# A hybrid attention block on one core: one gating weight's cast placed behind the cast of the keys' second slice

## The chip, the core and the metric

The kernel runs on one core of a Trainium2 chip. The core has five engines that run their own instruction streams: PE (TensorE, matrix products), DVE (VectorE), ACT (ScalarE), POOL (GpSimd) and SP (SyncE, which here only issues transfers). They wait for each other through semaphores, and each works through its own instructions strictly in the order in which they were built. The metric is the device time of one execution in microseconds (us); lower is better. A program was profiled once per version, and the profile is a record of one execution.

## The reference, cut to what matters

The layer projects 512 positions and 16 leading "meta" positions (528 in all) with one large weight `w_in`, runs two causal attention branches with 16 heads each beside each other, gates both and merges them.

```
u = rmsnorm(h)
proj = u @ w_in          # cq, ckv, k_pe, z_mla, fq, fk, fv, f_logit, z_fox, gate_a, gate_b
o_mla = attention(q_m, k_m, v_mla)                 # latent branch
y_mla = (o_mla * silu(z_mla)) @ w_br_mla
cum   = cumsum(log_sigmoid(f_logit + b))
o_fox = attention(fq, fk, fv, cum)                 # forgetting branch
y_fox = (o_fox * silu(z_fox)) @ w_br_fox
h = h + rmsnorm((sig(gate_a)*y_mla + sig(gate_b)*y_fox) @ w_out)
```

## The kernel before, in words

**Two-part products.** Every matrix product is done in three passes, since each fp32 operand is held as a rounded part (`h`) and a remainder (`l`): high by high, high by low, low by high. A weight slab of 128 x 1024 is loaded into `wraw`, ACT rounds it into `wh` (line 127, in `wsplit`), and POOL subtracts to get `wl` (line 102). The pools of `wraw`, `wh` and `wl` hold three slabs each, so a new load starts only when an older slab's `wl` is done, and a new cast only when PE has used an older `wh` for the last time. The same split is made of activations: ACT rounds (line 239, in `hl_done`) and DVE subtracts (line 102).

**Stages.** Heads are taken in pairs. There are 16 attention stages: for each pair `pr` from 0 to 7 first the forgetting branch (`br` = 1), then the latent branch (`br` = 0). PE is filled in all of them: while DVE and ACT work on the softmax of a stage, PE computes the projections that the next stages need (the list `fill`). A stage consists of `s0` (scores of the query blocks 0, 1, 2), the attention-times-values product `ov` of the stage before (`late`), `s1` (scores of block 3), and then the steps of `fill` with the softmax parts `n0` and `n1` among them. For a forgetting stage the list is: one transposing transfer of the values, eight steps of its own gate `z_unit(1, pr)`, two of the latent queries `mq`, four of the latent gate `z_unit(0, pr)`, and so on; the twelfth step, `fill[11]`, is the first one of the latent gate, and it is this step that calls for the cast of the latent gate's weight. For a latent stage the list ends with the second slice of the next forgetting stage's keys `fk` (columns 272 to 527), right before that stage's `s0`.

**Order.** PE runs in the order written in the program. For ACT, DVE and POOL a scheduler at build time sets the order from priorities, and may pull an instruction far ahead of the place where it is written. `tc.issue_after(x)` tells the scheduler that an instruction must stand behind `x` on its engine; the list `behind` holds such an `x` for the casts in `wsplit`, and `halved[key, i]` remembers the cast of slice `i` of a stage's queries or keys. Transfers are all issued by SP, one after the other: weight loads, the transposing transfers of the softmax numerators (`pt<-pn`, eight in each stage) and of the values (`vp<-vh`), and small loads.

In the scores of `s0`, block 0 reads keys 0 to 143 (matmuls of 144 columns), block 1 keys 0 to 271, block 2 keys 0 to 399. So the first two need the first slice of the keys alone, and the third, with 400 columns, is the first reader of the second slice: its rounded part from ACT, and for the last two of its six key matmuls the remainder from DVE. DVE reads the finished scores out of PSUM (line 755), ACT takes exponentials (line 763), ACT and DVE scale and split them (lines 790, 791).

Of the kernel before, what the change touches and what calls it, by code (L numbers as in the profile page):

```python
# [54 lines left out]
def block_kernel(ctx: ExitStack, tc: tile.TileContext, x, meta_tokens, pre_norm_g, w_in, fox_forget_b,  # L55
# [29 lines left out]
    behind, through, first_t, exps, halved = [], [], [], [], {}  # L85
# [126 lines left out]
    def run(steps):  # L212
        for _, fn in steps:
            fn()
# [309 lines left out]
    def gate_unit():  # L524

        i, br = gates.pop(0)

        def done(_, ps):
            ths[i, br] = thp.tile([128, S], F32, tag="th", name=f"th{i}{br}")
            nc.scalar.activation(ths[i, br], ps, AF.Tanh, scale=0.5)  # L530
        return unit(f"pg{i}{br}", win_w((O_GA, O_GB)[br], i), u_act, KD, REAL, done)


    with ExitStack() as att:
# [289 lines left out]
        def feed(br, pr):  # L824

            q = (q_mla, q_fox)[br](pr)
            k = (k_mla, k_fox)[br](pr)
            v, vts[br, pr] = v_unit(br, pr)
            return q, k, v
# [13 lines left out]
        for si, (br, pr) in enumerate(stages):  # L843
            last = si + 1 == len(stages)
            if not last:
                q, k, v = feed(*stages[si + 1])
            if br == 1:

                za, zb = z_unit(1, pr), z_unit(0, pr)
                fill = (vts[br, pr] if pr else begun) + za + q + zb[:4] + k + zb[4:6] + v + zb[6:]  # L850
            elif not last:

                fill = vts[br, pr] + q + k[:KD] + v + k[KD:]
            else:
                g = gate_unit()
                fill = vts[br, pr] + g + gate_unit() + gate_unit()
# [9 lines left out]
        for si, (br, pr) in enumerate(stages):  # L866
            s0, s1, n0, n1, va = attention(br, pr)

            for fn in [s0] + late + [s1]:
                fn()  # L870

            fill = fills[si]
            if si == 0:

                run(fill[:5])
                run(vts[1, 0] + pe_rest)
                n0()
                n1()
                first_t.extend(through)
                run(fill[5:])  # L880
            else:
                run(fill[:1])
                if si == 1:

                    written[0] = True
                    for x in range(2):
                        store0(x, 2, 8)
                    written[0] = False
                run(fill[1:5])
                if si == 1:  # L890

                    behind[:] = exps[:1]
                if si == 2:
                    behind.clear()
                n0()
                run(fill[5:12])
                n1()
                if 6 <= si < 8:

                    written[0] = True  # L900
                    rest1(si - 6)
                    written[0] = False
                run(fill[12:])
            written[0] = False
            if si == 1:

                behind[:] = [halved[("k", 1, 1), 0]]
            late = [va]
# [146 lines left out]
```

## Time and profile before

| what | value |
|---|---|
| median of 3 runs | 625.7 us (625.54 to 627.62) |
| span of the profiled execution, first to last instruction | 622.1 us |
| PE busy | 599.9 us, 96% of the span |
| ACT busy | 330.8 us, 53% |
| DVE busy | 315.4 us, 51% |
| POOL busy | 265.5 us, 43% |
| attention stages | about 67 us to 421 us of the span |

The profile page gives a span for the profiled execution and no other time of its own; the median of the runs is 3.6 us above that span, which holds what lies ahead of the first and behind the last instruction of the program. A timeline row of the profile reads: start in us from the span's start, duration, engine, line, operation, output tile <- input tiles with shapes, count, and in brackets the time for which the engine sat idle just before it and what ended that wait. A row of the chain of waits reads: start, duration, what the time belongs to.

### The profile page before, as it was taken

To read this page: it belongs to the slowest core of one execution; us is meant where nothing else is said; L and a number is where in the kernel's file an instruction comes from. 1 tells how busy PE (TensorE), PEld (TensorE's weight loads), DVE (VectorE), ACT (ScalarE), POOL (GpSimd) and SP (SyncE) were. 2 spreads that over 40 slices of the span, in tenths; PEclk is the share of its full clock that TensorE was granted. 3 is DMA by queue.
4 is the path that set the end of the run, shared out by engine and by line. 5 is a ranking of instruction groups with operands and counts; after the bars stand their busy time and mean duration, and the time that the engine had idled before them with its cause. 6 is when DMAs were issued, how large, how long until landed. Compare 5 with 4: busy or idle time off the path is not lost.

```text
span 622.1 us, 11008 instructions
## 1 busy us (share of the span) xinstructions
PE 599.9 (96%) x3811; PEld 507.3 (82%) x3811; DVE 315.4 (51%) x922; ACT 330.8 (53%) x757; POOL 265.5 (43%) x270
## 2 busy tenths in 40 slices
PE   5997999799999999999999999999999999999996
PEld 5886789689889789888888898887888888888885
DVE  3848647555765764674675657627321122024034
ACT  7755745655764864774676657656322222232321
POOL 4307535352346543344443523542744444444610
PEclk9999999899999999999999999999999999999999
DMA  9422589969798787878579697871433332333602
GB/s 289 99 76 53 120 178 142 242 141 190 145 186 161 149 208 154 172 167 204 140 161 174 145 169 159 187 168 40 136 102 101 102 93 79 100 103 115 257 34 102
DMA packets 223512, 89.31 MB, mean 144 GB/s; under 512 B 141708, under 2 KB 216852, under 8 KB 223456
## 3 DMA queue, kind: packets, MB, share of 16 engines
q1 hardware_dynamic: 223456, 88.61, 61.9%
q8 instruction: 30, 0.49, 0.3%
q14 instruction: 26, 0.21, 0.1%
HBM read 54.43 MB, written 4.00 MB: 94 GB/s over the span
## 4 chain that ended last, share of the span: by engine, by line
PE 86%; DVE 5%; ACT 4%; issue 2%; DMA 1%; SPq 0%; POOL 0%; DVEq 0%; ACTq 0%
PE z L96 14%; PE pg L96 14%; PE py L96 14%; PE v L96 9%; PE fq L96 7%; PE po L96 7%; PE fk L96 7%; PE st L96 5%; PE ov L96 3%; PE psm L96 3%; DVE sf L755 2%; PE mq L96 2%; ACT wh L127 2%; PE mk L96 1%; DVE vh L690 1%
## 5 line engine op out<-in xcount | busy, mean ns | idle before, releaser
L102 POOL TENSOR_TENSOR wl<-wraw,wh 128x1024 fp32r<-128x1024 f32 (+1 forms) x90 | 207.3, 2308 | 221.0 <-ACT wh L127 219.2
L127 ACT CAST wh<-wraw 128x1024 fp32r<-128x1024 f32 (+1 forms) x90 | 89.9, 1003 | 172.3 <-issue 47.7
L763 ACT ACTIVATE sf<-sf,nb 128x144 f32<-128x144 f32 (+3 forms) x128 | 72.0, 564 | 15.8 <-DVE nb L755 15.8
L791 DVE SCALAR_TENSOR_TENSOR pn<-sf,ri,pn 128x128 f16<-128x128 f32 (+3 forms) x128 | 68.8, 576 | 13.1 <-ACT pn L790 12.2
L790 ACT ACTIVATE pn<-sf,ri 128x128 f16<-128x128 f32 (+3 forms) x128 | 61.5, 551 | 19.9 <-ACT sf L763 17.9
L938 DVE SCALAR_TENSOR_TENSOR tb<-th,py 128x512 f32<-128x512 f32 x16 | 11.0, 687 | 101.9 <-PE py L96 101.9
L96 PE MATMUL st<-hlk,hlq 64*128 64x272 f32 (+3 forms) x480 | 52.8, 317 | 5.0 <-ACT hlk L239 4.1
L96 PE MATMUL z<-uTh,wh 128*128 128x512 f32 x128 | 50.8, 397 | 0.0
L96 PE MATMUL pg<-uTh,wh 128*128 128x512 f32 x128 | 50.2, 392 | 0.0
L96 PE MATMUL z<-uTh,wl 128*128 128x512 f32 x128 | 50.1, 391 | 0.0
L96 PE MATMUL z<-uTl,wh 128*128 128x512 f32 x128 | 49.9, 390 | 0.0
L96 PE MATMUL pg<-uTh,wl 128*128 128x512 f32 x128 | 49.8, 389 | 0.0
L96 PE MATMUL pg<-uTl,wh 128*128 128x512 f32 x128 | 49.8, 389 | 0.0
L96 PE MATMUL py<-gh,wh 128*128 128x512 f32 x128 | 49.8, 389 | 0.0
L96 PE MATMUL py<-gl,wh 128*128 128x512 f32 x128 | 49.8, 389 | 0.0
L96 PE MATMUL py<-gh,wl 128*128 128x512 f32 x128 | 49.8, 389 | 0.0
L96 PEld LDWEIGHTS st<-hlk,hlq 64*128 64x128 f32 x480 | 37.0, 186 | 15.0 <-ACT hlk L239 5.8
L755 DVE CUSTOM_DVE_ANT_0 sf<-st,maskt 128x272 f32<-128x272 f32 (+2 forms) x128 | 48.4, 434 | 0.9 <-PE st L96 0.8
L777 POOL TENSOR_TENSOR mt<-sf,ri 128x96 f32<-128x96 f32 (+1 forms) x32 | 9.5, 297 | 89.4 <-DVE ri L772 66.5
L96 PE MATMUL v<-uTh,wh 128*128 128x256 f32 (+1 forms) x128 | 36.6, 286 | 2.3 <-DVE hlk L102 2.3
L96 PE MATMUL v<-uTl,wh 128*128 128x256 f32 (+1 forms) x128 | 36.5, 285 | 0.0
L96 PE MATMUL fk<-uTl,wh 128*128 128x256 f32 (+1 forms) x128 | 36.4, 285 | 0.0
(189 smaller groups left out, 1403.3 us busy)
## 6 DMA issues: line engine op xcount, KB each, us to landing
wraw<-in_w_in_dram SPq DMA_DIRECT2D x56, 512.0 KB
wraw<-in_w_br_fox_dram SPq DMA_DIRECT2D x8, 512.0 KB
wraw<-in_w_br_mla_dram SPq DMA_DIRECT2D x8, 512.0 KB
wraw<-in_w_out_dram SPq DMA_DIRECT2D x8, 512.0 KB
pt<-pn SPq DMA_TRANSPOSE x128
xr<-in_x_dram SPq DMA_DIRECT2D x4, 512.0 KB
out_dram<-yo SPq DMA_DIRECT2D x8, 256.0 KB
QP<-qpe_dram SPq DMA_DIRECT2D x7, 256.0 KB
```

The source lines that it names most:

```text
L96: nc.tensor.matmul(*a, **k)
L102: eng.tensor_tensor(out=lo, in0=src, in1=f32(hi), op=ALU.subtract)
L127: nc.scalar.copy(wh[:, :n], raw[:, :n])
L690: nc.vector.scalar_tensor_tensor(out=lo, in0=p, scalar=sc[:, 3:4], in1=hi, op0=ALU.mult, op1=ALU.subtract)
L755: nc.vector.tensor_tensor_reduce(out=sf_of(h, b)[:, c0 : c0 + w], in0=ps[h][:, o : o + w], in1=maskt[:, m0 : m0 + w], scale=-scale, scalar ...
L763: exps[g] = nc.scalar.activation(sf, sf, AF.Exp, bias=sums["nb"][:, h, b : b + 1], scale=-1.0, accum_out=sums["su"][:, h, b : b + 1]).ins
L777: nc.gpsimd.tensor_tensor(out=mt, in0=src, in1=ri.unsqueeze(3).broadcast_to([128, 2, nb_, META]), op=ALU.mult)
L790: nc.scalar.activation(hi, sf, AF.Copy, scale=rib)
L791: nc.vector.scalar_tensor_tensor(out=lo, in0=sf, scalar=rib, in1=hi, op0=ALU.mult, op1=ALU.subtract)
L938: nc.vector.scalar_tensor_tensor(out=tb[br], in0=ths[i, br], scalar=1.0, in1=py, op0=ALU.add, op1=ALU.mult)
```

## The change

The twelfth step of `fill` is taken out of the run of seven steps and run by itself. In forgetting stages, while it runs, `behind` holds the cast of the keys' second slice of this same pair, so that the cast of the latent gate's weight, which this step calls for, must stand behind that cast on ACT. The change acts in stages after the first one, so on pairs 1 to 7.

```diff
                 n0()
-                run(fill[5:12])
+                run(fill[5:11])
+                if br:
+
+                    behind[:] = [halved[("k", 1, pr), 1]]
+                run(fill[11:12])
+                if br:
+                    behind.clear()
                 n1()
```

On ACT, around the end of the latent stage of pair 1 and the start of the forgetting stage of pair 2, the order changes as follows (`wh_2185` is the latent gate's weight of pair 2, `hlk_1907` the forgetting keys of pair 2, `fk_1980` their second slice in PSUM, `sf` the scores):

```order
 L687 ACTIVATE vh<-v_1916,vsc_1941 128x2x128
 L687 ACTIVATE vh<-v_1943,vsc_1941 128x2x128
-L127 COPY wh_2185<-wraw_1914 128x1024 [waits DMAHW5_49,PE_49]
 L239 COPY hlk_1907<-fk_1980 128x256 [waits PE_49]
+L127 COPY wh_2185<-wraw_1914 128x1024 [waits DMAHW5_49]
 L763 ACTIVATE sf_2012,su_2010<-sf_2012,nb_2009 128x144 [waits DVE_49]
 L763 ACTIVATE sf_2012,su_2010<-sf_2012,nb_2009 128x272 [waits DVE_49]
```

The weight's cast and the cast of the second key slice have changed places, and nothing else on ACT has moved there; the same exchange stands in each of the seven pairs. The weight's cast no longer names PE, since the cast ahead of it already waits for the same end of the key projection.

On PE, at the first use of that weight, two steps after the gate of the stage's own branch:

```order
 L96 MATMUL mq_2174<-cTl,wh_2168 128x512
 L96 MATMUL mq_2174<-cTh,wl_2169 128x512
-L96 MATMUL z_2195<-uTh,wh_2185 128x512
+L96 MATMUL z_2195<-uTh,wh_2185 128x512 [waits Activation_49]
 L96 MATMUL z_2195<-uTl,wh_2185 128x512
 L96 MATMUL z_2195<-uTh,wl_2186 128x512 [waits Pool_49]
```

The order of PE is the same; the first matmul with the latent gate's weight now has a wait of its own for ACT, since the wait for the key cast no longer covers it. DVE, POOL and SP keep their order.

## The prediction

> **What bounds the kernel now.** I read the page first. It says that PE is the engine to look at: whatever PE loses in a stage is lost for the whole.
>
> ```profile
> PE 599.9 (96%) x3811; PEld 507.3 (82%) x3811; DVE 315.4 (51%) x922; ACT 330.8 (53%) x757; POOL 265.5 (43%) x270
> ```
>
> Second, the chain of waits in order of time, at the border between the latent stage of pair 1 and the forgetting stage of pair 2. It runs on PE with one excursion:
>
> ```profile
> 155.66 2.77 PE fk L96 x23
> ...
> 158.46 1.05 ACT wh L127
> 159.51 0.27 ACT hlk L239
> ...
> 159.83 1.09 PE st L96 x8
> 160.92 1.97 PE ov L96 x26
> ...
> 171.12 2.74 PE z L96 x12
> ```
>
> The keys' second slice leaves PE at 158.46, and then the weight's cast runs, then the keys' cast, and only then the scores of 400 columns. Third, the list of waits, to see how often this happens and how much PE sits still for it (total us, times, longest):
>
> ```profile
> PE st L96 <- ACT hlk L239: 4.1, 6, 3.3
> PEld st L96 <- DVE hlk L102: 1.0, 6, 0.2
> ACT wh L127 <- PE fk L96: 2.7, 6, 0.5
> ```
>
> PE waits once for 3.3 us (pair 1) and briefly in the later pairs, of which one falls under what this list counts. Six weight casts start at the very moment at which the key projection ends, because they wait for a slot that this projection still holds. So the weight's cast, which nobody needs soon, and the keys' cast, which PE needs within a microsecond, are released by the same event, and the wrong one stands first. Fourth, the timelines of ACT and DVE there:
>
> ```profile
> 158.46 1.05 ACT L127 CAST wh<-wraw 128x1024 fp32r<-128x1024 f32 x1 [0.46 <-PE fk L96]
> 159.41 0.36 ACT L239 CAST hlk<-fk 128x256 fp32r<-128x256 f32 x1
> 160.49 0.42 ACT L763 ACTIVATE sf<-sf,nb 128x144 f32<-128x144 f32 x1 [0.71 <-DVE nb L755]
> 157.67 1.02 DVE L690 SCALAR_TENSOR_TENSOR vh<-v,vsc,vh 128x16 f16<-128x16 f32 x3 [0.72 <-ACT vh L687]
> 159.81 0.42 DVE L102 TENSOR_TENSOR hlk<-fk,hlk 128x256 fp32r<-128x256 f32 x1 [1.12 <-ACT hlk L239]
> ```
>
> **The change, term by term. First, six stages (pairs 2 to 7).** Nothing is added or removed; two ACT instructions change places. The weight's cast holds ACT for 0.95 us (158.46 to 159.41). Without it ahead, the keys' cast starts at 158.46 and DVE, free since 158.69, starts the remainder 0.40 later (159.41 to 159.81 now), at 158.86, and ends it at 159.28. When does PE want them? Its timeline in this stage, and below it the same three groups in the first forgetting stage, where the keys were ready long before:
>
> ```profile
> 158.47 0.56 PE L96 MATMUL st<-hlk,hlq 64*128 64x144 f32 x6
> 158.97 0.59 PE L96 MATMUL st<-hlk,hlq 64*128 64x272 f32 x6
> 159.83 0.91 PE L96 MATMUL st<-hlk,hlq 64*128 64x400 f32 x6
> 160.57 0.34 PE L96 MATMUL st<-CT,ONE 64*128 64x400 f32 x2
> 160.85 2.04 PE L96 MATMUL ov<-pt,vp 80*64 80x512 f16 x26
> ...
> 67.18 0.58 PE L96 MATMUL st<-hlk,hlq 64*128 64x272 f32 x6
> 67.73 0.72 PE L96 MATMUL st<-hlk,hlq 64*128 64x400 f32 x6
> 68.27 0.36 PE L96 MATMUL st<-CT,ONE 64*128 64x400 f32 x2
> ```
>
> Unhindered, the group of 400 follows the group of 272 after 67.73 - 67.18 = 0.55, and its last two matmuls follow after 68.27 - 67.73 = 0.54. Here the distances are 0.86 and 0.74. So PE loses 0.31 waiting for the rounded part and 0.20 waiting for the remainder, 0.51 in all. Unhindered, PE would want the rounded part at 159.52; it would be there at about 158.88 (PE now starts 0.42 after the cast's start). The remainder would end at 159.28, and its first reader, the fifth of the six key matmuls, comes after 159.52. Both are early by more than 0.2, so the whole 0.51 goes: 6 x 0.51 = **3.06**. The chain of waits has the same pieces in all six pairs.
>
> What pays for it? The weight's cast starts about 0.38 later (the keys' cast, 0.36 long, now lies ahead of it), and POOL's subtraction with it. SP in turn often waits for that subtraction before it issues the next load (us, times, longest):
>
> ```profile
> 159.59 2.38 POOL L102 TENSOR_TENSOR wl<-wraw,wh 128x1024 fp32r<-128x1024 f32 x1 [1.80 <-ACT wh L127]
> ...
> SPq L90 <- POOL wl L102: 167.4, 46, 14.7
> ```
>
> The subtraction then ends near 162.35 instead of 161.97. The first matmul with that weight stands at 171.12 (chain above, minus 0.51 now): over 8 us of cover, so I cost the new wait on PE at nothing. Without the cover it would be 0.38 a stage. Behind the cast on ACT stand the exponentials; they start at 160.49 now because DVE was held by the remainder. With DVE early they are free to start when the cast ends, about 159.8, that is 0.7 sooner. Behind POOL's subtraction SP waits with the next weight load, and behind that load, in SP's queue, stand the transposing transfers of the stage, which the next `ov` waits for. They start from exponentials that come 0.7 sooner, so in most stages they are early too. One place is tight: in the latent stage of pair 4 `ov` starts 268.63 - 265.64 = 2.99 after the last transfer's issue, against 180.29 - 176.09 = 4.20 in pair 2:
>
> ```profile
> 265.64 1.30 SPq L90 DMA_TRANSPOSE pt<-pn  x1
> 268.63 0.62 PE L96 MATMUL ov<-pt,vp 80*64 80x512 f16 x4
> ...
> 176.09 1.33 SPq L90 DMA_TRANSPOSE pt<-pn  x1
> 180.29 2.04 PE L96 MATMUL ov<-pt,vp 80*64 80x512 f16 x26
> ```
>
> There PE may not use its 0.51. I charge **-0.2** (bounds 0 and -0.51, since I cannot see whether SP or the softmax sets that row).
>
> **Second, pair 1.** Here the weight's cast did not wait for PE but for its own load, and held the keys back with it:
>
> ```profile
> 109.63 4.28 DMA wraw<-in_w_in_dram
> 113.99 1.04 ACT L127 CAST wh<-wraw 128x1024 fp32r<-128x1024 f32 x1 [3.63 <-DMA wraw<-in_w_in_dram]
> ...
> 111.33 0.59 PE L96 MATMUL st<-hlk,hlq 64*128 64x272 f32 x6
> 115.36 1.28 PE L96 MATMUL st<-hlk,hlq 64*128 64x400 f32 x6 [3.31 <-ACT hlk L239]
> 116.43 0.54 PE L96 MATMUL st<-CT,ONE 64*128 64x400 f32 x2
> 116.90 3.00 PE L96 MATMUL ov<-pt,vp 80*64 80x512 f16 x26
> 119.83 0.64 PE L96 MATMUL st<-hlk,hlq 64*128 64x272 f32 x6
> ...
> 112.46 1.61 SPq L90 DMA_TRANSPOSE pt<-pn  x1
> ```
>
> Now the group of 400 can start at 111.33 + 0.55 = 111.88 and be done near 112.7. It is tempting to book the whole 3.3. But `ov` stands next, and the last transposing transfer that it reads is issued only at 112.46. In pair 4 such a transfer had landed within 2.99 of its issue, the load just ahead in the same queue took 4.28; by these it lands between 115.45 and 116.74. I take the middle, 116.1. The wait moves from the keys to the transfer: `ov` starts 0.8 sooner, not 3.3.
>
> Then the clock. After the wait PE ran at half speed, as the stretches show (length, PE busy and count, the other engines, then the granted clock):
>
> ```profile
> 115.50:118.80 3.30, 3.30 (x18) 1.82 (x20) 2.51 (x13) 2.78 (x11) 1.98 (x1) 0.50 1.01 279
> 118.90:121.00 2.10, 2.10 (x35) 1.76 (x31) 1.42 (x4) 1.59 (x6) 1.16 (x4) 1.00 1.30 225
> ```
>
> So `ov` took 2.93 there (116.90 to 119.83) against 1.97 in pair 2. The new idle time, 112.7 to 116.1, is about as long as the old one. If the half-speed stretch comes again and lies on `ov` from its start, its 3.4 us do the work of 1.7, 0.27 is left at full speed, and `ov` ends at 119.77: a gain of 0.1. If it does not come, `ov` ends at 118.07: 1.8. I take **0.8**, the earlier start with the slow `ov` as it is now, between those ends.
>
> [...]
>
> **Sum** against the profiled execution: 3.06 - 0.2 + 0.8 = 3.66 from a span of 622.1: 618.4. The median of the runs lies 3.6 above the span; I leave that as it is: **622.0 us**, 0.6% faster.
>
> **The rivals.** *The clock stays up in pair 1.* For it: the gap shrinks a little. Against it: a gap of 3.31 in the rows was enough before, and the new one is no shorter by more than my error. Gain 3.06 + 1.8 = 4.9, no loss in pair 4: 620.8; with the transfer landing at 115.45 another 0.6, so 620.2.
>
> *The gain is eaten by the next wait.* The stalls go, but only the 0.31 of the rounded part are kept, since DVE has something else in hand when the cast ends early, or the transfers of other latent stages don't follow; and pair 1 gives 0.1. For it: transfers and DVE are in order and busy. Against it: DVE is idle for 1.12 before the remainder now. 6 x 0.31 + 0.1 = 2.0: 623.7; down to 1.1 where two or three stages give nothing: 624.6. That the change doesn't do what it says belongs here (the keys' cast gated by something other than the weight's cast), but the ACT rows leave no gap between the two.
>
> *Slower: the weight's late subtraction holds SP.* In each stage SP's next load waits for POOL's subtraction, 0.38 later, and the transfers behind it in the queue slip by as much, while PE comes 0.51 sooner: 0.89 of cover is used up. If a transfer then takes the 4.28 of the load above in five latent stages, PE stalls 4.28 - 4.20 + 0.89 = 0.97 in each, and 0.89 in pair 4: 5.7, against 3.06 + 0.8 saved: 627.6. It decides from a landing time over 3.3, and makes the whole slower when the stall exceeds 0.64 a stage. Against it: the transfers wait for exponentials that come sooner, and pair 4 shows landings within 2.99.
>
> **How the numbers follow.** About 0.5% (3.1 us) is what a measurement of this kernel can tell from no change. Forecast 0.60, its own range 621.0 to 623.3; about 0.47 of it is over 3.1. Clock stays up 0.20, all of it over. Eaten 0.16, all within 0.5%. Slower 0.04. So faster 0.67, same 0.29, slower 0.04. The range for 8 in 10 reaches from the first rival's 620.3 to the second's 624.6.
>
> **What would show it.** Right: no row "PE st <- ACT hlk" of pairs 2 to 7, the group of 400 following that of 272 after 0.55, `ov` 1.87 after the first scores in place of 2.38; in pair 1 an idle stretch of PE ahead of `ov` and not ahead of the scores. Wrong: stalls on `ov` in the latent stages, exponentials that don't start sooner, or a pair 1 in which `ov` starts at 113 or at 117.

## The result

| | time, us (lowest to highest, runs) |
|---|---|
| before | 627.17 (625.54 to 627.62, 6) |
| changed | 622.12 (620.02 to 624.50, 6) |
| ratio | 0.9938, 95% interval 0.9918 to 0.9959 |

The ratio is the estimate on record; the quotient of the two medians, which lie 5.05 us apart, is 0.992. The changed kernel is 0.6% faster by this measurement, and the first experiment below shows how much of such a ratio is not the change's. Its profiled execution took 622.67 us with a span of 620.9. The page's span and its busy time by engine:

```profile
span 620.9 us, 11001 instructions
PE 598.2 (96%) x3811; PEld 508.3 (82%) x3811; DVE 315.9 (51%) x922; ACT 330.6 (53%) x757; POOL 265.2 (43%) x270
```

Each of these engines runs as many instructions as before; PE has 1.7 us less of busy time. Three rows from the list of waits of the changed kernel (total us, times, longest):

```profile
PE ov L96 <- DMA pt<-pn: 3.5, 2, 3.1
...
ACT wh L127 <- DMA wraw<-in_w_in_dram: 3.3, 1, 3.3
...
PE st L96 <- DVE nb L755: 0.2, 1, 0.2
```

"PE st <- ACT hlk", which stood at 4.1 us in six waits, has left the list. In its place PE waits 3.5 us for the transposed numerators. ACT still waits for the weight's load, but now with nothing urgent behind it.

Now the border between the latent stage of pair 1 and the forgetting stage of pair 2. This is the timeline of PE in the changed kernel:

```profile
160.35 0.56 PE L96 MATMUL st<-hlk,hlq 64*128 64x144 f32 x6
...
160.86 0.58 PE L96 MATMUL st<-hlk,hlq 64*128 64x272 f32 x6
161.28 0.28 PE L96 MATMUL st<-CT,ONE 64*128 64x272 f32 x2
161.40 0.72 PE L96 MATMUL st<-hlk,hlq 64*128 64x400 f32 x6
161.96 0.34 PE L96 MATMUL st<-CT,ONE 64*128 64x400 f32 x2
162.23 2.04 PE L96 MATMUL ov<-pt,vp 80*64 80x512 f16 x26
```

And ACT and POOL at the same place:

```profile
160.46 0.37 ACT L239 CAST hlk<-fk 128x256 fp32r<-128x256 f32 x1 [0.57 <-PE fk L96]
160.73 1.05 ACT L127 CAST wh<-wraw 128x1024 fp32r<-128x1024 f32 x1
162.06 0.42 ACT L763 ACTIVATE sf<-sf,nb 128x144 f32<-128x144 f32 x1 [0.28 <-DVE nb L755]
161.87 2.37 POOL L102 TENSOR_TENSOR wl<-wraw,wh 128x1024 fp32r<-128x1024 f32 x1 [2.19 <-ACT wh L127]
```

The group of 400 follows the group of 272 after 161.40 - 160.86 = 0.54, and its last two matmuls come 0.56 later: no stall. `ov` stands 162.23 - 160.35 = 1.88 behind the first scores, against 2.38 before. From the first scores of one forgetting stage to those of the next, the pairs 2 to 6 took 45.35, 42.99, 43.01, 42.99 and 42.98 us before, and 44.84, 42.47, 42.48, 42.47 and 42.47 now: 0.51 to 0.53 less in each. From the first scores of pair 2 to the first output projection (`po`) it is 413.94 before and 410.86 now, a gain of 3.08.

Pair 1 went the other way. Its PE timeline, and two stretches of the view by windows (length, PE busy and count, PEld, DVE, ACT and POOL likewise, granted clock, DMA share, GB/s):

```profile
112.61 0.72 PE L96 MATMUL st<-hlk,hlq 64*128 64x400 f32 x6
113.16 0.35 PE L96 MATMUL st<-CT,ONE 64*128 64x400 f32 x2
116.65 0.61 PE L96 MATMUL ov<-pt,vp 80*64 80x512 f16 x1 [3.14 <-DMA pt<-pn]
117.59 3.79 PE L96 MATMUL ov<-pt,vp 80*64 80x512 f16 x25 [0.33 <-DMA pt<-pn]
121.31 1.05 PE L96 MATMUL st<-hlk,hlq 64*128 64x272 f32 x6
...
122.90 0.50 PE L96 MATMUL z<-uTh,wh 128*128 128x512 f32 x1
```

```profile
112.00:115.40 3.40, 1.51 (x22) 1.17 (x18) 2.77 (x14) 0.06 (x2) 0.12 (x1) 1.00 0.91 203
115.50:122.20 6.70, 5.22 (x34) 3.73 (x36) 1.15 (x4) 6.19 (x19) 3.50 (x5) 0.50 1.20 268
```

The scores of 400 columns no longer wait (113.51 is their end), and PE then sits still for 3.14 us ahead of `ov`. The granted clock was 0.50 for some 6.7 us, twice the 3.3 us of the profile before, so `ov` took 116.65 to 121.31. Pair 1 took 48.79 us to the first scores of pair 2, against 47.65.

The two spans follow from these pieces. The first scores of pair 1 came 0.74 later in the changed kernel's execution (111.56 against 110.82; the first scores of all, 67.44 against 66.68, were already as late), pair 1 took 1.14 longer, the six stages 3.08 less, and from the first `po` to the end both took 49.7: 0.74 + 1.14 - 3.08 = -1.20, which is 620.9 against 622.1.

### The profile page after: what moved, and what is told of

It is laid out like the page before. It is cut to its first block, busy times and chain, and to the rows that moved or that the text cites. A ratio compares the mean times of both kernels' runs of the same rounds, so it can differ in the third digit from the quotient of the medians.

```text
span 620.9 us, 11001 instructions
## 1 busy us (share of the span) xinstructions
PE 598.2 (96%) x3811; PEld 508.3 (82%) x3811; DVE 315.9 (51%) x922; ACT 330.6 (53%) x757; POOL 265.2 (43%) x270
## 4 chain that ended last, share of the span: by engine, by line
PE 85%; DVE 5%; ACT 3%; DMA 2%; issue 2%; SPq 1%; POOL 1%; DVEq 0%; ACTq 0%; POOLq 0%
PE pg L96 14%; PE py L96 14%; PE z L96 14%; PE v L96 8%; PE po L96 7%; PE fq L96 6%; PE fk L96 6%; PE st L96 5%; PE ov L96 3%; PE psm L96 3%; DVE sf L755 2%; PE mq L96 2%; SPq L90 1%; PE mk L96 1%; DMA ht<-in_x_dram 1%
## 5 line engine op out<-in xcount | busy, mean ns | idle before, releaser
L96 PE MATMUL st<-hlk,hlq 64*128 64x272 f32 (+3 forms) x480 | 51.0, 311 | 0.7 <-DVE nb L755 0.2
L96 PE MATMUL ov<-pt,vp 128*64 128x512 f16 (+4 forms) x416 | 35.2, 318 | 3.5 <-DMA pt<-pn 3.5
L96 PEld LDWEIGHTS <-vp 128*64 128x64 f16 (+1 forms) x416 | 22.8, 113 | 17.5 <-issue 8.5
```

The lines of the kernel that those rows point to most:

```text
L96: nc.tensor.matmul(*a, **k)
```

## Experiments

In each run the kernel is compared with runs of the kernel before on the same chip. Besides the times, two distances on PE are used, since they don't depend on when the execution began: from the first scores of a forgetting stage to its `ov`, and the two stretches "pair 1" (first scores of pair 1 to those of pair 2) and "rest" (from there to the first `po`). keys_late1 and keys_late3 were executed once each, the others several times.

**The two kernels once more, side by side: b_again (before) and a_again (changed), no edit.**

> The kernel before, unchanged, to see how its time goes with the half-speed stretches of the clock. Theory A (the six short stalls were worth 3.0 us, and pair 1 only changes where PE idles and how long it then runs at half speed): the executions differ by steps of about 1.7 us, the loss of one half-speed stretch of 3.4 us, and the mean granted clock falls by about 0.003 with each step. Rival B (the spread comes from the transfers, not from the clock): times differ at the same granted clock.

> The changed kernel, unchanged, as the mark for the partial versions. Theory A: ratio to before 0.992 to 0.996, and again steps of about 1.7 us that go with the granted clock. Rival B: no such steps.

b_again: 624.06 us (623.13 to 625.57, 8 runs), ratio 0.9959 [0.9941, 0.9978] to the runs of the very same program beside it, at 627.0. a_again: 621.79 (621.3 to 624.0, 6), ratio 0.9926 [0.9904, 0.9948]. So a ratio to those reference runs has 0.4% in it that has nothing to do with the change. The direct ratio of the two medians is 621.79 / 624.06 = 0.9964, 2.3 us.

Most of it goes with the granted clock. Each execution comes with its mean clock, and the times follow:

| mean clock | kernel before, mean us (runs) | changed, mean us (runs) |
|---|---|---|
| 0.996 | 623.75 (11) | 621.14 (4) |
| 0.992 | 625.78 (16) | 622.03 (4) |
| 0.989 | 627.41 (12) | 624.25 (2) |

The half-speed stretch in pair 1 of the profile before took 3.41 us at a clock of 0.50 (115.48 to 118.89). By the author's estimate it costs half of that, 1.7 us, of PE work and lowers the mean by 1.7 / 620 = 0.003, and executions differ by the number of such stretches. In the profiles, for example, before and b_again (0.996) have 3.4 us of half clock in pair 1, after and a_again (0.992) 6.8. Before and after have a further piece at the very end, from 620.65 and from 617.21 on, behind PE's last product (616.5 and 615.3), so it lowers the mean and costs PE nothing. The clock is not all, so the rival is not ruled out for the rest: at one and the same clock the times of before still differ, from 623.13 to 624.80 at 0.996 and from 624.68 to 627.84 at 0.992. The 13 executions between the rows of the table averaged 627.32 (0.991), 626.66 (0.993) and 624.90 (0.994), so the steps are not clean. One other part can be seen: the first scores of pair 1 begin between 109.8 and 113.3 us in the eleven profiled executions, with no edit ahead of them. The reference runs had a mean clock of 0.992 (44 runs), b_again 0.9945. Why the same program has a higher clock here than as the reference stays open. At equal clock the change is worth 2.6 to 3.8 us.

**The exchange in pairs 2 to 7 alone: swap_pairs2to7.**

```diff
-                if br:
+                if br and pr > 1:
```

(the same in the second `if br:`)

> The cast order is exchanged in pairs 2 to 7 only; pair 1 stays as before. Theory A: PE's marks gain 0.50 us in each of six forgetting stages, 3.0 us in all, and nothing in pair 1, where PE idles ahead of the scores as before; ratio to before 0.995. Rival C (the gain sits in pair 1, the only stage with a long idle time): ratio 0.999 to 1.001.

622.83 us (620.52 to 624.69, 9 runs), ratio 0.9949 [0.9928, 0.997]. First scores to `ov` is 1.88 in pairs 2 to 7, the rest 410.87, as in the changed kernel; pair 1 took 47.75, as before. The whole six-stage term stands by itself in these rows. The median alone would not show it: it lies only 1.2 us below b_again's 624.06, which by itself would suit rival C. At equal clock it does: the four executions at 0.991 averaged 624.36, the seven reference runs at 0.991 627.32.

**The exchange in pair 1 alone: swap_pair1.**

```diff
-                if br:
+                if br and pr == 1:
```

> The cast order is exchanged in pair 1 only. Theory A: the idle time of about 3.3 us moves from the scores to the values product, which waits for its last transposing transfer and starts 0.8 to 1.0 us sooner; the rest is the clock's, so minus 1.8 to plus 1.2 us in one execution and a ratio of 0.997 to 1.001 over several. Rival C: PE gains 3 us or more there, ratio 0.994 to 0.995.

623.96 us (620.94 to 628.12, 12 runs), ratio 0.9958 [0.9937, 0.9979], the same as b_again without any edit. The rest is 413.90, as before. At equal clock there is no gain either: 623.66 at 0.996 (3 runs) against 623.75. But the one profiled execution had a pair 1 of 45.77 us, 1.9 less than before, at the edge of what was expected. Its PE timeline, and the same stretch by windows:

```profile
114.09 0.38 PE L96 MATMUL ov<-pt,vp 80*64 80x512 f16 x1 [2.32 <-DMA pt<-pn]
115.02 2.01 PE L96 MATMUL ov<-pt,vp 80*64 80x512 f16 x25 [0.55 <-DMA pt<-pn]
```

```profile
115.50:118.80 3.30, 3.30 (x42) 2.80 (x39) 1.80 (x7) 2.79 (x10) 2.04 (x5) 1.00 1.04 272
```

Here the clock stayed at 1.00, and the 25 products of `ov` took 2.01 us, against 3.79 at 0.50 in the changed kernel. So the stall has really moved to the transfer and is shorter there, and what it is worth depends on the clock. Pair 1's first scores to its gate `z` took 11.34, 11.19 and 11.09 us in three profiled executions with the exchange (after, a_again and keys_late1), 9.69 in keys_late3 and 8.31 here; without it 10.18, 9.50 and 10.27 (before, b_again, swap_pairs2to7). The means are 10.3 and 10.0: no gain that these few executions show.

**How early are the keys? keys_late1 and keys_late3: one or three extra copies of the keys' second slice on ACT, ahead of its cast, in pairs 2 to 7.** The result is the same, each copy only takes time (0.40 us).

```diff
+                if key[0] == "k" and key[1] == 1 and key[2] > 1 and i == 1:
+                    for _ in range(1):
+                        nc.scalar.copy(hl[:, 0, o : o + w_], ps)
```

(`range(3)` in keys_late3)

> As the changed kernel, with the keys' cast of the second slice done twice over in pairs 2 to 7 (one extra copy of 128x256 ahead of it on ACT, some 0.4 us). Theory A with the slack of the prediction (rounded part there 0.64 us before PE wants it): nothing is lost, PE's distance from the first scores to the values product stays at 1.88 us in these stages. Rival D (the gain came from something that starts earlier with the cast, exponentials or transfers): each stage loses about the 0.4 us.

> As the changed kernel, with three extra copies ahead of the keys' cast in pairs 2 to 7 (1.1 to 1.4 us). Theory A: the first 0.64 us are free, the rest comes back as a stall, with about 0.2 more for the remainder: 0.65 to 1.0 us in each of six stages, a distance of 2.5 to 2.9 us from the first scores to the values product. Rival D: 1.1 to 1.4 us a stage.

One execution each: 622.33 us (clock 0.994) and 626.26 us (0.994). PE at the border of pair 2, first with one copy, then with three:

```profile
159.99 0.58 PE L96 MATMUL st<-hlk,hlq 64*128 64x272 f32 x6
...
160.53 0.80 PE L96 MATMUL st<-hlk,hlq 64*128 64x400 f32 x6
161.16 0.34 PE L96 MATMUL st<-CT,ONE 64*128 64x400 f32 x2
```

```profile
160.28 0.91 PE L96 MATMUL st<-hlk,hlq 64*128 64x400 f32 x6 [0.54 <-ACT hlk L242]
```

With one copy the group of 400 still follows after 0.54, and only its last two matmuls come 0.07 late (0.63 after its start instead of 0.56): the rounded part was still early, the remainder just not, so `ov` came 1.95 to 1.96 after the first scores and not 1.88 as expected. With three copies the keys' cast starts 1.32 after the first scores instead of 0.11, 1.21 late. The group of 400 starts 160.28 - 158.54 = 1.74 after the first scores instead of 161.40 - 160.35 = 1.05, so 0.69 late (the 0.54 in the row counts only the time in which PE sat idle). The rounded part had thus been 1.21 - 0.69 = 0.52 early. `ov` comes 2.76 to 2.77 after the first scores, 0.88 later than without copies. Both margins are thus measured: about 0.52 for the rounded part, about 0.33 for the remainder (0.40 late cost 0.07). The second one alone gives the loss: the remainder starts 1.20 late with three copies, and 1.20 - 0.33 = 0.87; in the kernel before it started 1.34 after the first scores (159.81 - 158.47) instead of 0.52 (160.87 - 160.35), 0.82 late, and 0.82 - 0.33 = 0.49. Rival D is out: one copy of 0.40 cost 0.07 a stage.

**Fill the gap in pair 1: fill_the_gap, scores_first, block3_first.** All three are the changed kernel with PE's order altered in the forgetting stage of pair 1 (`si == 2`), so that PE has work while the transfer is under way: four gate steps ahead of `ov`; the scores of block 3 and two gate steps; the scores of block 3 alone.

```diff
-            for fn in [s0] + late + [s1]:
-                fn()
+            if si == 2:
+                s0()
+                s1()
+                late[0]()
+            else:
+                for fn in [s0] + late + [s1]:
+                    fn()
```

This is block3_first. In scores_first `run(fill[1:3])` stands between `s1()` and `late[0]()`; in fill_the_gap `s0()` is followed by `run(fill[1:5])`, `late[0]()` and `s1()`. The steps run ahead are not run a second time.

> As the changed kernel, and in the forgetting stage of pair 1 four steps of the stage's own gate (12 matmuls of 512 columns, 2.8 us) are done ahead of the values product that waits for its transfer. Theory A: PE has work through most of the wait, so 2.6 to 2.9 us of it are saved and the clock is not lowered: 4 to 6 us off the changed kernel's profiled execution, span 615 to 617, ratio to before 0.984 to 0.988. Rival E (the values product waits for something that PE's own progress releases, and the wait moves along): no gain, ratio as the changed kernel's 0.994.

> As the changed kernel, and in the forgetting stage of pair 1 the scores of block 3 and two steps of the stage's own gate (2.6 us of matmuls) stand ahead of the values product that waits for its transfer. In fill_the_gap the wait was covered, but DVE took the scores of block 3 up later and PE lost 2.1 us ahead of the latent keys. Theory F (PE's wait for the transfer is covered and DVE and ACT get the scores of block 3 early): from the first scores of pair 1 to the last product's first matmul 453.5 to 454.5 us, against 456.3 in fill_the_gap, no half-speed stretch there; ratio to before 0.984 to 0.989. Rival G (DVE and ACT are held up again behind the values product): 456 us or more, ratio 0.990 to 0.994.

> As scores_first without the two gate steps: the scores of block 3 alone (1.2 us of matmuls) stand ahead of the values product. [...] Rival G: as the changed kernel, 0.993.

| | time, us (runs) | ratio to before | pair 1, us | rest, us |
|---|---|---|---|---|
| a_again | 621.79 (6) | 0.9926 [0.9904, 0.9948] | 48.65 | 410.88 |
| fill_the_gap | 620.97 (6) | 0.9913 [0.9884, 0.9942] | 45.43 | 410.89 |
| scores_first | 618.77 (6) | 0.9888 [0.9862, 0.9913] | 45.81 | 411.02 |
| block3_first | 618.50 (6) | 0.9888 [0.9863, 0.9913] | 44.48 | 410.90 |

In all three the clock of the profiled execution was 1.00 from 112.0 to 125.6, where the changed kernel's was 0.50 for 6.83 us, and the last two beat both kernels: about 3 us below the changed kernel, or 0.4% by the ratios (a_again was measured beside other reference runs, and the intervals overlap a little). The first two give part of it back at another place. fill_the_gap fell short of what was expected of it (0.984 to 0.988). scores_first has the ratio of its theory F but not its mark: from the first scores of pair 1 to the first `po` it took 45.81 + 411.02 = 456.8 us, where 453.5 to 454.5 was expected and 456 or more was the mark of rival G; fill_the_gap took 456.3, block3_first 455.4. Over the whole of the profiled execution the clock was 0.997 in fill_the_gap and 0.996 in scores_first, against 0.998 in block3_first. With the gate's steps earlier, the order of DVE's work changed too, and PE then waited for DVE (its list of waits):

```profile
PE mk L96 <- DVE sil L704: 1.4, 1, 1.4
...
PE mk L96 <- DVE hlq L102: 0.6, 1, 0.6
```

In scores_first the wait came back at the next `ov`, of the latent stage (its PE timeline):

```profile
136.07 0.38 PE L96 MATMUL ov<-pt,vp 80*64 80x512 f16 x1 [0.72 <-DMA pt<-pn]
137.50 2.01 PE L96 MATMUL ov<-pt,vp 80*64 80x512 f16 x25 [1.04 <-DMA pt<-pn]
```

block3_first has neither, and its `ov` of pair 1 waits only 0.36, where the 2.9 of the gaps in after and a_again (the mean of 3.14 and 2.61) less the 1.2 of block 3's scores (119.83 to 121.00 in the kernel before) would leave 1.7 (PE timeline, then the windows):

```profile
115.42 0.40 PE L96 MATMUL ov<-pt,vp 80*64 80x512 f16 x1
116.18 2.01 PE L96 MATMUL ov<-pt,vp 80*64 80x512 f16 x25 [0.36 <-DMA pt<-pn]
118.12 0.50 PE L96 MATMUL z<-uTh,wh 128*128 128x512 f32 x1
```

```profile
112.00:115.40 3.40, 2.95 (x30) 2.10 (x26) 2.98 (x17) 1.43 (x4) 0.30 (x1) 1.00 1.17 275
115.50:118.80 3.30, 2.94 (x29) 2.12 (x30) 1.18 (x6) 3.30 (x13) 2.13 (x2) 1.00 1.02 300
```

First scores to gate `z` is 118.12 - 111.09 (its first scores) = 7.03, against 11.34 in the changed kernel. So the gap ahead of `ov` and the half clock around it were indeed what pair 1 had lost in that execution.

## Why the prediction was right, and where it was not

**The six stages: right in place and size.** Predicted 0.51 a stage and 3.06 in all; measured 0.50 from the first scores to `ov`, 0.51 to 0.53 from stage to stage, and 3.08 in all (413.94 to 410.86), and swap_pairs2to7 has it alone. The rounded part was put at 0.64 early (159.52 - 158.88) and measured at about 0.52: the keys' cast did not start with the first scores (158.46 against 158.47 in the prediction) but 0.11 behind them (160.46 against 160.35). It was early all the same. For the remainder, the prediction said no more than that its first reader comes after 159.52, 0.24 behind its end; the margin is about 0.33.

**Pair 4's charge of -0.2: nothing was paid.** From the first scores to `ov` the latent stages took 2.29 to 2.30 before and after. The transposing transfers were not what set that row.

**The cover for the weight: right.** POOL's subtraction starts 161.87 - 160.35 = 1.52 after the first scores instead of 1.12, 0.40 later (0.38 was expected), and PE has no wait for that weight.

**The exponentials: right direction, half the size.** Expected 0.7 sooner; measured 162.06 - 160.35 = 1.71 after the first scores against 160.49 - 158.47 = 2.02, so 0.31 sooner. ACT is free at 161.78, as thought, but then waits 0.28 for DVE's `nb`, which the step left out. It cost nothing.

**Pair 1: right mechanism, wrong size.** As predicted, the wait moved from the keys to the last transposing transfer, and `ov` did not come 3.3 sooner: it came 116.65 - 111.56 = 5.09 after the first scores, against 116.90 - 110.82 = 6.08 (110.82 is when pair 1's scores begin in the profile before), so 1.0 sooner where 0.8 was predicted. The term that was mis-sized is "the slow `ov` as it is now": the term allowed for one half-speed stretch, as before, at the worst for a gain of 0.1. In three of the five profiled executions with the exchange (after, a_again, keys_late1) the half clock lasted 6.8 us in place of 3.4, and the longer stretch took back more than the 1.0 in the first of them. The term of +0.8 measured -1.1 in the profiled pair (47.65 to 48.79) and -0.3 between the means over eight profiles, which is no gain and no clear loss. Its upper end of 1.8 came up once, in swap_pair1 (47.65 to 45.77).

**The base: wrong, and the error helped.** "The median of the runs lies 3.6 above the span" mixed different executions, and what lies ahead of the first and behind the last instruction is not 3.6. Every execution with both figures lies 1.74 to 1.86 us above its own span (622.67 - 620.9 = 1.8). The profiled execution of before had a mean clock of 0.996; at 622.1 + 1.8 = 623.9 it was quicker than each of the three runs (625.54 to 627.62), whose clocks are not on record. The predicted sum, read correctly, was 618.4 + 1.8 = 620.2 for an execution at 0.996, where the changed kernel has 621.14: about 0.9 too quick, the same size as pair 1's missing 0.8. That 622.0 and 622.12 agree so closely is partly luck, as two errors of the sum worked against each other.

**The rivals.** The one in which the clock stays up in pair 1 was real in single executions: swap_pair1 had it in its profile at clock 0.999, which makes it one in five of the profiled executions with the exchange in pair 1. The gain was not eaten by the next wait in the six stages: the whole 0.50 was kept, not the 0.31 of the rounded part. The slower rival, SP held by the later subtraction, is refuted by the unchanged 2.29 of the latent stages and the 1.88 of all six forgetting stages.

**What is left open:** the measured 0.62% is more than the 3 us (0.5%) that the rows account for, and the 0.36% between a_again and b_again is less; the reference runs' lower clock can supply the first difference, but why they have it was not found. Why the keys' cast starts 0.12 later against the first scores than the weight's cast did in its place was not found either.

## What to carry to other kernels

When two instructions of one engine are released by the same event, look at which of them has a reader on the critical path at once: here the order alone was worth half a microsecond a stage, and its size could be read from two start-to-start distances, one in a hindered stage and one in an unhindered one. When a long wait is removed, ask where the next operand is at that moment: moving a wait from one matmul to the next is worth little, and filling it with work whose operands are there (block 3's scores) was worth about as much as the six stages together, 0.4% against 0.5%. Before a profile is set against a median, compare their mean clocks: a profile of one execution belongs to the executions with its own clock.

## What the runs showed of the hardware

**Half clock came with gaps of 2.50 to 3.55 us in pair 1, and not with one of 2.32.** PE sat still for 3.14 us in the changed kernel and for 2.61 in a_again, and in b_again for only 2.50. This is the wait in b_again, and the clock behind it:

```profile
114.71 1.07 PE L96 MATMUL st<-hlk,hlq 64*128 64x400 f32 x6 [2.50 <-ACT hlk L239]
```

```profile
115.50:118.80 3.30, 3.30 (x20) 1.46 (x20) 1.99 (x12) 3.01 (x12) 1.34 (x1) 0.51 1.04 288
```

The half clock came each time: in b_again from about 115.3 on, 0.6 behind the gap's end at 114.71, in the changed kernel from 115.45 on, 1.20 ahead of the gap's end at 116.65, and there PE had been busy for 1.51 of the 3.40 us before it (window 112.00 to 115.40 above). In swap_pair1, which has the same order in pair 1 as the changed kernel, the clock stayed at 1.00 with a gap of 2.32 and a second one of 0.55. So the same place can go either way. These are all eleven profiled executions (gaps from the PE timelines; times of the half clock that are marked "about" are worked out from the mean clock of the windows over its ends):

| run | gaps of PE in pair 1, us | half clock, us |
|---|---|---|
| swap_pairs2to7 | 3.55 | about 114.9 to 118.3 |
| before | 3.31 | 115.48 to 118.89 |
| after | 3.14, 0.33 | 115.45 to 122.28 |
| a_again | 2.61, 0.33 | about 115.1 to 121.9 |
| keys_late1 | 2.56, 0.33 | about 115.0 to 121.8 |
| keys_late3 | 2.54, 0.34 | about 115.8 to 119.2 |
| b_again | 2.50 | about 115.3 to 118.7 |
| swap_pair1 | 2.32, 0.55 | none (1.00 from 112.0 to 125.6) |
| block3_first | 0.36 | none (1.00 from 112.0 to 125.6) |
| scores_first | 0.20 | none (1.00 from 112.0 to 125.6) |
| fill_the_gap | none listed | none (1.00 from 112.0 to 125.6) |

Elsewhere in the kernel before, a gap of 2.28 us ahead of `v` (it ends at 57.90) was followed by a clock of 1.00 (57.90 to 61.30). No run changed the length or the place of a gap by itself, so what decides between the two outcomes was not shown.

**The half clock lasted 3.4 us in some executions and 6.8 in others.** With the stall of 0.33 us inside it, the changed kernel stayed at 0.50 for 6.83 us; in keys_late3, with a stall of 0.34 inside it, it was 3.4, as in before, b_again and swap_pairs2to7 without one. What makes the difference was not shown, and no run tested it by itself.
